# Layer 0 of a two-layer encoder trunk: another order of the inverse's partitions, fewer reads, and roots with reciprocals in PSUM

## The chip, the core and the metric

The kernel runs on one core of a Trainium2 chip. The core has a TensorE (matrix products, written PE; its weight loads are PEld), a VectorE (DVE), a ScalarE (ACT), a GpSimd (POOL) and a SyncE (SP), which here issues nearly all DMAs. Each engine has its own instruction queue and works through it in order; engines wait for each other by semaphores. SBUF is the on-chip memory of 128 partitions, PSUM the accumulator memory that TensorE writes. The metric is the device time of one execution in microseconds (us). Lower is better.

## The reference

The reference is one inference step of a trunk with two layers, for a prompt of 512 tokens and a sample of 32 tokens that carries state. Layer 0 mixes tokens by an RWKV-7 recurrence, layer 1 by differential attention; both also have memory attention and a gate, and one output projection.

What matters for the change is layer 0's recurrence over 24 heads of size 64:

```python
kk = kk / jnp.maximum(jnp.linalg.norm(kk, axis=-1, keepdims=True), 1e-12)
...
sa = jnp.einsum('bhvk,bhk->bhv', S, -kk_t)
S = (S * w_t[:, :, None, :] + sa[..., None] * (kk_t * a_t)[:, :, None, :]
     + v_t[..., None] * k_t[:, :, None, :])
y_t = jnp.einsum('bhvk,bhk->bhv', S, r_t)
...
y = (y - mean) * lax.rsqrt(var + GN_EPS) * ln_w + ln_b
```

The kernel handles it by chunks of 64 tokens. Inside a chunk the `sa` rows depend on each other through a strictly triangular matrix, so the kernel needs the inverse of a unit triangular matrix of 64 by 64 for each chunk and head. It inverts the diagonal blocks of 32 by 32 by elimination and joins two of them by products. It also needs two kinds of inverse square roots: of the norms of `kk`, and of the variances of `y`.

## The kernel before

The 24 heads are worked through as 12 pairs (two heads fill 128 partitions). While the chunk chain of pair `pr` runs, the kernel prepares pairs `pr + 1` to `pr + 3` and finishes pair `pr - 1`. All of it is interleaved by hand with the big matrix products of the input projection, which are done in three passes of float32r (`hh*whi`, `hl*whi`, `hh*wlo`); these fill TensorE wherever the chain leaves room. Each product's result is a half of a block, 128 by 272, accumulated in a PSUM buffer named `ps_g`, from a ring of three buffers (`psg`); ScalarE and VectorE empty it.

The order of layer 0 is written out: `PLAN` has, for each of the 24 steps of a pair's chain, what is done beside it; `Queue` and `tie` chain the instructions of TensorE, VectorE, ScalarE and SyncE in the order in which the program issues them. GpSimd's instructions are not chained in this way; they are placed by the framework's scheduler. In layer 1 the scheduler orders all engines.

The steps that matter here are:

- `rw_prep` makes a pair's triangular blocks `at` and writes the blocks to be inverted to DRAM as `sc1`: 34 blocks of 32 by 32 (32 of the prompt, 2 of the sample).
- "inv" is `rw_invert`: SyncE reads `sc1` into the tile `m3` on 102 partitions, each block three times (three classes, `NCL`), and GpSimd runs the elimination: each block's 32 columns are divided among the three classes (column `n` belongs to class `n mod 3`), and 31 steps of a product into `tm` (L861) and a sum into `u3` (L863) follow. `u3` starts as a copy of `ui`, which holds ones at each class's columns.
- "back" is `rw_back`: SyncE writes `u3` to DRAM (`sc2`), class by class. "at" is `rw_at`: SyncE reads it back into `at`. "mrg" is `rw_merge`: VectorE transposes blocks into `t1b`, TensorE joins two inverted blocks (`ps_w`), ScalarE copies.
- "rsq" computes both kinds of roots in one call: `q20` is a tile of 128 by 26, 16 columns of sums of squares of `kk` from `rw_prep` and 10 columns of variances from `rw_finish`; the result is `r20`. In the profile both have the name `q`, and the temporary tile is `nt`. The call is `self.rsqrt` with eight VectorE instructions, each of which reads what the one ahead of it wrote. It happens 16 times: once for each of the first three pairs in the lead-in, once in step 17 of each of the 12 chains, and once in the tail.
- "fin" is `rw_finish`: after "rsq" comes the multiplication of `yt` by `r20` on VectorE, then TensorE's transposes into `ps_y`, then the gate. Also `rw_prep` reads `r20`: it splits 16 columns into `rr`, which TensorE transposes into `ps_rt`.

Before the change the three classes of the 32 prompt blocks lie on partitions 0 to 31, 32 to 63 and 64 to 95, and those of the two sample blocks on 96 to 101. So `rw_invert` issues six DMAs, two for each class. `consts_rwkv` builds the class of each partition, `cls`, by five comparisons of the partition's number with 32, 64, 96, 98 and 100, and from it `ui`.

`self.rsqrt` begins with an estimate from the exponent bits and has two polynomial steps. Other calls of it (input norms, layer 1) are not touched.

The tail of layer 0 (`TAIL`) is one more "rsq" and the last "fin" steps, in the middle of the last gate's product; directly after it the output projection starts, which opens two `ps_g` buffers at once.

Of the kernel before, what the change touches and what calls it, by code (L numbers as in the profile page):

```python
# [9 lines left out]
F32 = mybir.dt.float32  # L10
F32R = mybir.dt.float32r
BF16 = mybir.dt.bfloat16
I32 = mybir.dt.int32
AF = mybir.ActivationFunctionType
ALU = mybir.AluOpType
AX = mybir.AxisListType

P = 128
# [72 lines left out]
NCL = 3  # L91
NBLK = 34
# [16 lines left out]
class Trunk:  # L109
# [21 lines left out]
    def rsqrt(self, y, x, pool, tag):  # L131
# [10 lines left out]
        self.ve.scalar_tensor_tensor(t[:], t[:], -10.0 / 3.0 * f ** 2, t[:], ALU.add, ALU.mult)  # L142
        self.ve.scalar_tensor_tensor(y, t[:], 5.0 * f ** 4, y, ALU.add, ALU.mult)

    def params(self, p, name, rows, queue=None):

        t = p.tile([P, P], F32, name=name)
        r0 = 0
        for src, n in rows:
            (queue or self.se).dma_start(t[r0 : r0 + n, :], src)  # L150
            r0 += n
        return t, r0
# [34 lines left out]
    def consts_rwkv(self, c):  # L187

        nc, a = self.nc, self.a

        mk = c.tile([P, 2, P], BF16, name="mk")
        self.mk = mk
        nc.gpsimd.memset(mk[:], 1.0)
        for par in range(2):
            for half in range(2):
                strict = (half == 1) if par == 0 else (half == 0)
                for rb in (0, 64):
                    v = mk[rb : rb + 64, par, half * 64 : half * 64 + 64]
                    nc.gpsimd.affine_select(
                        out=v, in_=v, pattern=[[1, 64]], compare_op=ALU.is_gt if strict else ALU.is_ge,  # L200
                        fill=0.0, base=0, channel_multiplier=-1)

        self.hsel = c.tile([P, 34], F32, name="hsel")
        nc.gpsimd.memset(self.hsel[:], 0.0)
        nc.gpsimd.memset(self.hsel[:64, 2:3], 1.0)
        nc.gpsimd.memset(self.hsel[64:, 3:4], 1.0)
        self.hblk = c.tile([P, P], F32, name="hblk")
        nc.gpsimd.memset(self.hblk[:], 0.0)
        nc.gpsimd.memset(self.hblk[:64, :64], 1.0)
        nc.gpsimd.memset(self.hblk[64:, 64:], 1.0)  # L210

        self.hs4 = c.tile([P, 5, P], F32R, name="hs4")
        t4 = self.rp.tile([P, 5, P], F32, tag="rkv", name="t4", bufs=RKV)
        for c0, n, base in ((0, 4, 0), (4, 1, -2)):
            nc.gpsimd.iota(t4[:, c0 : c0 + n], pattern=[[-4, n], [-1, 2], [0, 64]], base=base, channel_multiplier=1,
                           allow_small_or_imprecise_dtypes=True)
        t5 = self.rp.tile([P, 5, P], F32, tag="rkv", name="t5", bufs=RKV)
        self.ve.tensor_scalar(t5[:], t4[:], 0.0, None, ALU.is_equal)
        self.ve.scalar_tensor_tensor(self.hs4[:], t4[:], float(NS), t5[:], ALU.is_equal, ALU.add)

        self.smask = c.tile([P, CW], BF16, name="smask")
        nc.gpsimd.memset(self.smask[:], 1.0)
        nc.gpsimd.memset(self.smask[:].rearrange("p (c w) -> p c w", w=65)[:, :, 0:1], 0.0)

        nr = (32 + NCL - 1) // NCL
        self.nr = nr
        self.ui = c.tile([NCL * NBLK, nr, 32], BF16, name="ui")
        ii = self.rp.tile([NCL * NBLK, nr, 32], F32, tag="rkv", name="ii", bufs=RKV)

        cl = c.tile([NCL * NBLK, 1], F32, name="cl")  # L230
        nc.gpsimd.iota(cl[:], pattern=[[0, 1]], base=0, channel_multiplier=1, allow_small_or_imprecise_dtypes=True)
        cls = c.tile([NCL * NBLK, 1], F32, name="cls")
        self.ve.tensor_scalar(cls[:], cl[:], 32.0, None, ALU.is_ge)
        for at, w in ((64, 1.0), (96, -2.0), (98, 1.0), (100, 1.0)):
            cl2 = c.tile([NCL * NBLK, 1], F32, name=f"cl{at}")
            self.ve.tensor_scalar(cl2[:], cl[:], float(at), None, ALU.is_ge)
            self.ve.scalar_tensor_tensor(cls[:], cl2[:], w, cls[:], ALU.mult, ALU.add)
        nc.gpsimd.iota(ii[:], pattern=[[NCL, nr], [-1, 32]], base=0, channel_multiplier=0,
                       allow_small_or_imprecise_dtypes=True)
        self.ve.tensor_scalar(self.ui[:], ii[:], cls[:, 0:1], 0.0, ALU.add, ALU.is_equal)  # L240
        self.SB = [[c.tile([P, P], F32, name=f"SB{i}{j}") for j in range(2)] for i in range(2)]
        self.SS = [c.tile([P, P], F32, name=f"SS{i}") for i in range(2)]
        for t in self.SB + [self.SS]:
            for u in t:
                nc.gpsimd.memset(u[:], 0.0)
        self.shc = c.tile([P, 2, NPROJ], F32, name="shc")
        self.nlam = self.c.tile([P, 1], F32, name="nlam")

        for t in self.zr[:2] + [self.bk]:
            self.pads(t)  # L250
        nc.gpsimd.memset(self.avz[:], 0.0)
        for t in self.svs:
            nc.gpsimd.memset(t[:], 0.0)
        nc.gpsimd.memset(self.q20[:], 1.0)
        nc.gpsimd.memset(self.uz[:].bitcast(F32), 0.0)
        nc.gpsimd.memset(self.rr[:].bitcast(F32), 0.0)
# [584 lines left out]
    def rw_invert(self, st):  # L841

        nc, p, sc1 = self.nc, self.rb, st["sc1"]
        if st["pr"] == 1:
            m3 = self.sg2[: NCL * NBLK, :1024].rearrange("p (s t) -> p s t", t=32)
            u3 = self.rk0.tile([P, 10, 64], F32, tag="gsq", name="u3r", bufs=1)
            u3 = u3[: NCL * NBLK].rearrange("p a b -> p (a b)")[:, : self.nr * 32].rearrange("p (n t) -> p n t", t=32)
        else:
            m3 = p.tile([NCL * NBLK, 32, 32], F32, tag="m3", name="m3", bufs=1)[:]
            u3 = p.tile([NCL * NBLK, self.nr, 32], F32, tag="u3", name="u3", bufs=1)[:]  # L850
        st["u3"] = u3
        for q in range(NCL):
            self.se.dma_start(m3[q * 32 : q * 32 + 32], sc1[:32])
            self.se.dma_start(m3[96 + 2 * q : 98 + 2 * q], sc1[32:])
        nc.gpsimd.tensor_copy(u3, self.ui[:])
        tm = p.tile([NCL * NBLK, self.nr, 32], F32, tag="tm", name="tm", bufs=1)
        for kx in range(31):
            n = kx // NCL + 1
            wd = 31 - kx
            sh = [NCL * NBLK, n, wd]  # L860
            nc.gpsimd.tensor_tensor(tm[:, :n, :wd], u3[:, :n, kx : kx + 1].to_broadcast(sh),  # L861
                                    m3[:, kx : kx + 1, kx + 1 :].to_broadcast(sh), ALU.mult)
            nc.gpsimd.tensor_tensor(u3[:, :n, kx + 1 :], u3[:, :n, kx + 1 :], tm[:, :n, :wd], ALU.add)  # L863

    def rw_back(self, st):

        u3 = st["u3"]
        st["sc2"] = [self.dp.tile([m, 32, 32], F32, tag=f"sc2{m}", name=f"sc2{m}", bufs=2) for m in (32, 2)]
        for o, t in zip((0, 96), st["sc2"]):
            m = t.shape[0]  # L870
            for q in range(NCL):
                n = len(range(q, 32, NCL))
                self.se.dma_start(t[:, q : 32 : NCL, :], u3[o + q * m : o + q * m + m, :n, :])

    def rw_at(self, st):

# [557 lines left out]
    def layer0(self, mem):  # L1434
        nc, o = self.nc, self.o
        w = self.a["rw_in"][0]
# [4 lines left out]
        with ExitStack() as ctx:  # L1441
# [23 lines left out]
            def go(kind, pr):  # L1465

                if kind == "rsq":
                    self.rsqrt(self.r20[:], self.q20[:], self.rk0, "nt")
                elif 0 <= pr < NPAIR:
                    if kind in ("inv", "back", "at"):  # L1470
                        {"inv": self.rw_invert, "back": self.rw_back, "at": self.rw_at}[kind](sts[pr])
                        return
                    if (kind, pr) not in run:
                        it = run[kind, pr] = self.rw_prep(sts[pr], rkv[pr]) if kind == "prep" else make[kind](sts[pr])
                        next(it)
                    next(run[kind, pr], None)
# [96 lines left out]
            for k, n in enumerate(FILL0):  # L1573
                go("prep", 0)
                if k == 3:
                    go("rsq", 0)
                if k == 26:
                    go("inv", 0)
                fill(n)
# [27 lines left out]
            for pr in range(NPAIR):  # L1607
# [9 lines left out]
                t, left, spent = 0.0, each[pr] - kept, 0.0  # L1617
# [56 lines left out]
        with ExitStack() as ctx:  # L1674
            p = self.pool("wo0", 1, ctx=ctx)
# [66 lines left out]
            for i in range(5):  # L1742
                n = P if i < 4 else TS
                dg = p.tile([P, P], F32, tag="dg", name="dg", bufs=2)
                self.ve.tensor_scalar(dg[:], self.ident[:], rs[:, i : i + 1], None, ALU.mult)
                c = i % 4 * P
# [490 lines left out]
```

## Time and profile before

| | |
|---|---|
| median of 3 runs | 1403.26 us (1402.6 to 1403.94) |
| the profiled execution: its time, its span | 1402.28 us, 1400.5 us |
| TensorE busy | 1361.5 us, 97% of the span |
| VectorE, ScalarE, GpSimd busy | 934.6, 828.6, 371.7 us |
| layer 0, about | 0 to 705 us of the span |
| granted TensorE clock | 0.996 |

How to read it: a row of a timeline has the start in us from the span's start, the duration in us, the engine, the line, the operation, the tiles as out<-in, the shape, and in square brackets the idle time of the engine just before it with what ended it. Nearly all instructions bear the line L106, that of the helper that issues them, so tiles' names tell them apart. A row of waits has the engine and tile that waited, what it waited for, and then us in total, times, and the longest in us. A group's row ends with its count, total busy us and mean ns of one. In a row by tile the three numbers are the shortest, median and longest duration in ns. SPq is SyncE's queue, with the time that it took to issue a DMA. Matmuls overlap, so two rows of PE can cover the same time.

### The profile page before, as it was taken

Reading aid. Unit: us, or ns where it says so; the run is one execution under the profiler, and the core shown is the slowest. Engines: PE = TensorE matmul, PEld = TensorE weight load, DVE = VectorE, ACT = ScalarE, POOL = GpSimd, SP = SyncE. Lnnn points to the kernel's source line nnn. Section 1 sums busy time; section 2 is a strip of 40 time slices with the busy share of each in tenths; the row PEclk is TensorE's granted clock in tenths of the full one; section 3 lists DMA queues with packets and bytes.
Section 4 is the critical chain, followed back from the end, with each engine's and each line's share of the span. In section 5 each row is a group of like instructions: output and inputs, shape, how many; then the busy total and the mean of one; then the engine's idle time right before and its main releaser. Section 6 shows DMA issues by size and latency. Waiting matters only on the chain.

```text
span 1400.5 us, 31939 instructions
## 1 busy us (share of the span) xinstructions
PE 1361.5 (97%) x11893; PEld 1296.7 (93%) x11893; DVE 934.6 (67%) x2345; ACT 828.6 (59%) x2304; POOL 371.7 (27%) x841
## 2 busy tenths in 40 slices
PE   8999999999999999999999999999999999999997
PEld 6988899999998998897899999999999999999997
DVE  5765777787877787676753476676467756767443
ACT  5756677767776777565543366664466546665222
POOL 2136567555865576520000040000000001001000
PEclk9999999999999999999999999999999999999999
DMA  7543222332233222342474473333333322332321
GB/s 224 155 118 80 49 57 76 84 96 62 67 82 99 61 77 73 87 131 64 121 206 118 120 218 108 92 92 93 101 92 94 104 73 84 97 106 84 91 76 72
DMA packets 264036, 139.45 MB, mean 100 GB/s; under 512 B 57721, under 2 KB 252802, under 8 KB 263882
## 3 DMA queue, kind: packets, MB, share of 16 engines
q1 hardware_dynamic: 263818, 137.41, 34.9%
q8 instruction: 94, 1.54, 0.5%
q14 instruction: 60, 0.49, 0.1%
q10 hardware_dynamic: 64, 0.02, 0.0%
HBM read 111.12 MB, written 22.91 MB: 96 GB/s over the span
## 4 chain that ended last, share of the span: by engine, by line
PE 81%; DVE 8%; ACT 3%; issue 2%; POOL 2%; DMA 2%; SPq 1%; DVEq 0%; ACTq 0%; POOLq 0%
PE ps_g L106 57%; PE ps_c L106 4%; PE ps_s L106 2%; PE ps_o L106 2%; PE ps_at L106 2%; DVE wlo L106 1%; PE ps_v L106 1%; SPq L106 1%; PE ps_mm L106 1%; PE ps_mo L106 1%; POOL tm L861 1%; PE ps_aT L106 1%; PE ps_yc L106 1%; POOL u L863 1%; PE ps_kv L106 1%
## 5 line engine op out<-in xcount | busy, mean ns | idle before, releaser
L106 PE MATMUL ps_g<-hh,whi 128*128 128x272 f32 x1808 | 541.0, 300 | 0.4 <-DVE memk L106 0.2
L106 PE MATMUL ps_g<-hh,wlo 128*128 128x272 f32 x1808 | 536.0, 297 | 1.6 <-DVE wlo L106 1.6
L106 PE MATMUL ps_g<-hl,whi 128*128 128x272 f32 x1808 | 532.1, 295 | 0.6 <-DVE hl L106 0.3
L106 PEld LDWEIGHTS ps_g<-hh,wlo 128*128 128x128 f32 x1808 | 341.7, 189 | 6.3 <-DVE wlo L106 2.3
L106 PEld LDWEIGHTS ps_g<-hh,whi 128*128 128x128 f32 x1808 | 341.9, 189 | 5.8 <-DVE og L106 0.6
L106 PEld LDWEIGHTS ps_g<-hl,whi 128*128 128x128 f32 x1808 | 341.8, 189 | 4.6 <-DVE hl L106 1.3
L106 DVE TENSOR_TENSOR wlo<-raw,whi 128x512 fp32r<-128x512 f32 x314 | 220.9, 714 | 123.0 <-ACT whi L106 119.2
L106 ACT CAST whi<-raw 128x512 fp32r<-128x512 f32 x314 | 189.1, 619 | 109.5 <-PE ps_g L106 61.4
L861 POOL TENSOR_TENSOR tm<-u,m 102x84 f32<-102x84 f32 (+23 forms) x341 | 143.7, 421 | 165.5 <-DMA m<-sc 139.7
L863 POOL TENSOR_TENSOR u<-u,tm 102x84 f32<-102x84 f32 (+23 forms) x341 | 148.3, 435 | 26.6
L106 PE MATMUL ps_g<-hi,whi 128*128 128x272 f32 x512 | 148.9, 291 | 0.0
L106 PE MATMUL ps_g<-hi,wlo 128*128 128x272 f32 x512 | 147.5, 288 | 0.5 <-DVE wlo L106 0.5
L106 PE MATMUL ps_g<-lo,whi 128*128 128x272 f32 x512 | 147.4, 288 | 0.0
L1333 POOL TENSOR_TENSOR lo<-og,hi 128x544 fp32r<-128x544 f32 x8 | 13.2, 1652 | 359.7 <-ACT hi L106 359.2
L106 PEld LDWEIGHTS ps_g<-hi,wlo 128*128 128x128 f32 x512 | 96.4, 188 | 0.8 <-DVE wlo L106 0.7
L106 PEld LDWEIGHTS ps_g<-hi,whi 128*128 128x128 f32 x512 | 96.4, 188 | 0.0
L106 PEld LDWEIGHTS ps_g<-lo,whi 128*128 128x128 f32 x512 | 96.4, 188 | 0.0
L106 ACT ACTIVATE pt<-ps_s,snm 128x128 f32<-128x128 f32 (+3 forms) x96 | 51.0, 532 | 41.7 <-DVE snm L106 41.6
L106 DVE SCALAR_TENSOR_TENSOR SB<-ps_c,dl,sd 64x64 f32<-64x64 f32 x168 | 47.4, 282 | 40.9 <-PE ps_c L106 37.7
L1754 POOL TENSOR_TENSOR hl<-hn,hh 128x544 fp32r<-128x544 f32 x8 | 12.5, 1567 | 211.3 <-ACT hh L106 211.2
L106 ACT ACTIVATE sg<-ps_g 128x272 f32<-128x272 f32 x64 | 25.3, 396 | 57.6 <-PE ps_g L106 53.0
L106 ACT COPY sv<-ps_c 64x64 f32<-64x64 f32 x192 | 39.5, 206 | 33.3 <-PE ps_c L106 31.2
(402 smaller groups left out, 2578.3 us busy)
## 6 DMA issues: line engine op xcount, KB each, us to landing
raw<-in_rw_in_dram SPq DMA_DIRECT2D x114, 256.0 KB
raw<-in_df_in_dram SPq DMA_DIRECT2D x112, 256.0 KB
raw<-in_w_out_dram SPq DMA_DIRECT2D x64, 256.0 KB
oscr<-sg SPq DMA_DIRECT2D x16, 272.0 KB
lo<-oscr SPq DMA_DIRECT2D x16, 272.0 KB
m<-sc SPq DMA_DIRECT2D x33, 128.0 KB
raw<-in_w_mem_v_dram SPq DMA_DIRECT2D x16, 256.0 KB
kh<-kh SPq DMA_DIRECT2D x24, 136.0 KB
```

Of the source, the lines that this page charges most:

```text
L106: return lambda *a, **k: self.trunk.tie(self, issue(*a, **k))
L861: nc.gpsimd.tensor_tensor(tm[:, :n, :wd], u3[:, :n, kx : kx + 1].to_broadcast(sh), m3[:, kx : kx + 1, kx + 1 :].to_broadcast(sh), ALU.mult)
L863: nc.gpsimd.tensor_tensor(u3[:, :n, kx + 1 :], u3[:, :n, kx + 1 :], tm[:, :n, :wd], ALU.add)
L1333: (self.nc.gpsimd if g % 2 and self.o1 else self.ve).tensor_tensor(lo[:], t, hi[:].bitcast(F32), ALU.subtract)
L1754: nc.gpsimd.tensor_tensor(self.hl[:, k, :], h[:], self.hh[:, k, :].bitcast(F32), ALU.subtract)
```

## The change

Three parts.

1. A block's three classes move to neighbouring partitions: partition `3 b + q` has class `q` of block `b`. `m3` is then read by two DMAs (prompt blocks and sample blocks), whose source repeats each block three times by a step of nothing. `rw_back` still issues six DMAs; each takes every third partition.
2. `consts_rwkv` gets `cls` in another way: two iotas on GpSimd write, for each partition, its distances from the starts of the blocks 1 to 33 into the tile `ii`; VectorE compares them with 0, sums them over the row, and so has the block's number; a third instruction gets the class. After that `ii` is written again, as before, for `ui`.
3. "rsq" calls the new `roots`. With x the input, u an estimate of the square root of x from its exponent bits, s = u + x/u (twice a Heron step), the result is about 1/s + s/(4 x), with a small factor on each part. The instructions are eight, on VectorE alone: the seed; `z` = 1/x; `w` = 1/u; `d` = `w` x; `u` = `d` + `u`; `w` = 1/`u`; `u` = 0.25 (1 - m) `u` `z`; out = (1 + m) `w` + `u`. `z`, `w` and `d` lie in PSUM, in a buffer of the ring `psg` in which the matrix products accumulate.

```diff
+    def roots(self):
+
+        x, out = self.q20[:], self.r20[:]
+        n = x.shape[1]
+        u = self.rk0.tile([P, n], F32, tag="nt", name="nt")[:]
+        ps = self.psg.tile([P, 512], F32, tag="g", name="ps_nt")
+        z, w, d = (ps[:, i * n : i * n + n] for i in range(3))
+        m = 3.0e-4
+        self.ve.tensor_scalar(u.bitcast(I32), x.bitcast(I32), 0.5, float(0x1FBB4F2E), ALU.mult, ALU.add)
+        self.ve.reciprocal(z, x)
+        self.ve.reciprocal(w, u)
+        self.ve.tensor_tensor(d, w, x, ALU.mult)
+        self.ve.tensor_tensor(u, d, u, ALU.add)
+        self.ve.reciprocal(w, u)
+        self.ve.scalar_tensor_tensor(u, u, 0.25 * (1.0 - m), z, ALU.mult, ALU.mult)
+        self.ve.scalar_tensor_tensor(out, w, 1.0 + m, u, ALU.mult, ALU.add)
...
         cls = c.tile([NCL * NBLK, 1], F32, name="cls")
-        self.ve.tensor_scalar(cls[:], cl[:], 32.0, None, ALU.is_ge)
-        for at, w in ((64, 1.0), (96, -2.0), (98, 1.0), (100, 1.0)):
-            cl2 = c.tile([NCL * NBLK, 1], F32, name=f"cl{at}")
-            self.ve.tensor_scalar(cl2[:], cl[:], float(at), None, ALU.is_ge)
-            self.ve.scalar_tensor_tensor(cls[:], cl2[:], w, cls[:], ALU.mult, ALU.add)
+        nc.gpsimd.iota(ii[:, 0, :], pattern=[[-NCL, 32]], base=-NCL, channel_multiplier=1, allow_small_or_imprecise_dtypes=True)
+        nc.gpsimd.iota(ii[:, 1, 0:2], pattern=[[-NCL, 2]], base=-33 * NCL, channel_multiplier=1,
+                       allow_small_or_imprecise_dtypes=True)
+        jj = ii[:].rearrange("p n t -> p (n t)")[:, : NBLK - 1]
+        self.ve.tensor_scalar(jj, jj, 0.0, None, ALU.is_ge)
+        self.ve.tensor_reduce(cls[:], jj, AX.X, ALU.add)
+        self.ve.scalar_tensor_tensor(cls[:], cls[:], -float(NCL), cl[:], ALU.mult, ALU.add)
         nc.gpsimd.iota(ii[:], pattern=[[NCL, nr], [-1, 32]], base=0, channel_multiplier=0,
                        allow_small_or_imprecise_dtypes=True)
         self.ve.tensor_scalar(self.ui[:], ii[:], cls[:, 0:1], 0.0, ALU.add, ALU.is_equal)
...
-        for q in range(NCL):
-            self.se.dma_start(m3[q * 32 : q * 32 + 32], sc1[:32])
-            self.se.dma_start(m3[96 + 2 * q : 98 + 2 * q], sc1[32:])
+        for b in (slice(0, 32), slice(32, NBLK)):
+            self.se.dma_start(m3[b.start * NCL : b.stop * NCL],
+                              sc1[b].unsqueeze(1).to_broadcast([b.stop - b.start, NCL, 32, 32]))
...
-                self.se.dma_start(t[:, q : 32 : NCL, :], u3[o + q * m : o + q * m + m, :n, :])
+                self.se.dma_start(t[:, q : 32 : NCL, :], u3[o + q : o + NCL * m : NCL, :n, :])
...
                 if kind == "rsq":
-                    self.rsqrt(self.r20[:], self.q20[:], self.rk0, "nt")
+                    self.roots()
```

## The prediction

> **What bounds the kernel now.** I read the page's busy line first, then the waits of TensorE, then the timeline around the longest class of them.
>
> ```profile
> span 1400.5 us, 31939 instructions
> ```
>
> ```profile
> PE 1361.5 (97%) x11893; PEld 1296.7 (93%) x11893; DVE 934.6 (67%) x2345; ACT 828.6 (59%) x2304; POOL 371.7 (27%) x841
> ```
>
> TensorE is the bound: it is busy for 1361.5 of 1400.5 us. None of the edits touches a matmul, so all they can win or lose lies in the other 39 us, where TensorE stood still. The view of waits says who held it:
>
> ```profile
> PE ps_y L106 <- DVE yt L106: 5.0, 10, 0.9
> PE ps_rt L106 <- DVE rr L106: 2.8, 1, 2.8
> PE ps_w L106 <- DVE t1b L106: 2.5, 5, 1.1
> ```
>
> All three stand behind something that the change touches. `ps_y` holds the transposes of a finished pair's outputs; they need `yt`, which VectorE multiplies by the roots `r20`, straight after the step "rsq". `ps_w` begins the merge of two inverted blocks, which waits for the inverse to come back from DRAM. VectorE's timeline in pair 1 and the TensorE row that waits for it:
>
> ```profile
> 208.14 0.17 DVE L106 TENSOR_SCALAR q<-gs 128x10 f32<-128x10 f32 x1
> 208.25 0.69 DVE L106 TENSOR_TENSOR wlo<-raw,whi 128x512 fp32r<-128x512 f32 x1
> ...
> 214.40 0.17 DVE L106 TENSOR_SCALAR q<-q 128x26 int32<-128x26 int32 x1
> ...
> 215.96 0.19 DVE L106 SCALAR_TENSOR_TENSOR q<-nt,q 128x26 f32<-128x26 f32 x1
> 216.06 0.73 DVE L106 TENSOR_TENSOR wlo<-raw,whi 128x512 fp32r<-128x512 f32 x1
> 216.72 0.85 DVE L106 TENSOR_TENSOR yt<-yt,q 128x640 f32<-128x640 f32 x1
> ```
>
> ```profile
> 217.72 0.74 PE L106 MATMUL ps_y<-ident,yt 128*128 128x128 f32 x5 [0.35 <-DVE yt L106]
> ```
>
> VectorE has no gap from 214.40 to the end of `yt` at 217.57, and TensorE resumes 0.15 us later after 0.35 us of waiting. So here the length of the roots sets when TensorE goes on, one to one. It is worse where GpSimd's elimination runs beside them (stretches of pair 1 and of a later pair, from the first to the last instruction of the roots; the columns are us, then PE, PEld, DVE, ACT and POOL busy):
>
> ```profile
> 214.40:216.15 1.75, 1.75 (x17) 1.75 (x16) 1.51 (x10) 1.68 (x6) 0.96 (x4) 1.00 0.20 55
> 443.37:445.41 2.04, 2.04 (x20) 2.04 (x18) 1.80 (x10) 1.97 (x7) 1.65 (x6) 1.00 0.14 40
> ```
>
> ```profile
> 447.14 0.63 PE L106 MATMUL ps_y<-ident,yt 128*128 128x128 f32 x4 [0.88 <-DVE yt L106]
> ```
>
> The same eight instructions take 1.75 us with 0.96 us of GpSimd beside them and 2.04 with 1.65, and TensorE's wait is 0.35 in the one and 0.88 in the other.
>
> **The change part by part.**
>
> **1. The roots.** Eight instructions before, eight after. Before, each waits for the one in front: 214.40 to 215.96 is seven steps of 0.22 us, the last ends 0.19 later, 1.75 in all. An instruction that waits for nothing starts after 0.11 (208.14 to 208.25). After: seed, `z`=1/x, `w`=1/u, `d`, `u`, `w`=1/u, `u`·`z`, out. `z` doesn't need the seed, and `u`·`z` doesn't need the second `w`. With old lengths that is five dependent steps (seed to `w`, `w` to `d`, `d` to `u`, `u` to `w`, `u`·`z` to out) of 0.22, one free step of 0.11 and an end of 0.19: 5 x 0.22 + 0.11 + 0.19 = 1.40; `z` lies inside the seed's step. Two prices are not in the trace at this size: a reciprocal of 26 columns, and a VectorE write to PSUM.
>
> ```profile
> L106 DVE RECIPROCAL mrs<-mrs 128x2 f32<-128x2 f32 x16 | 2.6, 165 | 6.9 <-ACT mp L106 6.8
> ...
> L106 DVE RECIPROCAL mrs<-mrs 128x1 f32<-128x1 f32 x8 | 1.3, 162 | 3.1 <-ACT mp L106 3.0
> ```
>
> ```profile
> L106 DVE RECIPROCAL mrs<-mrs x24: 152/166/168, 599.1 to 1154.2; 128x2 f32<-128x2 f32 x16, 128x1 f32<-128x1 f32 x8
> ```
>
> ```profile
> L106 DVE TENSOR_TENSOR tm_t<-tm_t,ps_n x4: 156/157/158, 1387.7 to 1393.2; 128x2 f32<-128x2 f32 x2, 128x3 f32<-128x3 f32 x2
> ...
> L106 DVE TENSOR_TENSOR tm_t<-fr x2: 160/161/162, 1388.1 to 1393.0; 128x2 f32<-128x2 f32 x1, 128x3 f32<-128x3 f32 x1
> ```
>
> ```profile
> L106 DVE MEMSET ps_s<- x96: 112/112/112, 844.0 to 1263.5; 64x64 f32 x96
> ```
>
> Mean to mean, a second column costs a reciprocal 3 ns: 165 + 24 x 3 = 237 ns for 26, against 190 for the step's old instruction. At the other end, from the shortest of the group to its longest, it is 16 ns a column: 168 + 24 x 16 = 552 ns. I take the means' side, where the two visible ones add 0.1 at most, and leave the step as it is. An input from PSUM made a multiplication 4 ns shorter (157 against 161), so PSUM reads are taken as equal. A write to PSUM lies between the memset's 112 ns and the old 190; I take the old. If the four writes (`z` is hidden) cost like the memset, three visible ones save 3 x 0.08 and the roots take 1.16. If instructions that touch the same PSUM bank also run one behind the other, `w` waits for `z` (0.11 more) and `u`·`z` for `w` (0.11 more): 1.62.
>
> [...]
>
> The roots stand in front of `yt` twelve times. Between the two stretches above the saving is 1.75 - 1.40 = 0.35 to 2.04 - 1.40 = 0.64, and the wait that it can remove is 0.35 to 0.88: they grow together. The ten waits hold 5.0 us, and I take four fifths of it, 4.0. (None of the new instructions takes two inputs from SBUF; whether that frees them of GpSimd no row shows, and if not, 0.2 of each long wait stays.) What is late next is the chain's own products `ps_c`, whose VectorE work moves forward with `yt`.
>
> **2. The matrices' reads.** SyncE issues six DMAs per pair before, two after, with the same bytes.
>
> ```profile
> 210.47 2.04 SPq L106 DMA_DIRECT2D m<-sc  x6
> ```
>
> ```profile
> 214.95 0.24 POOL L861 TENSOR_TENSOR tm<-u,m 102x31 f32<-102x31 f32 x1 [9.43 <-DMA m<-sc]
> ```
>
> At 2.04 / 6 = 0.34 each, SyncE is free 1.36 us sooner, and GpSimd's elimination, which starts 4.48 us after the first issue, starts up to 1.36 us sooner (nothing sooner if the bytes, not the issues, set it). In steady pairs no TensorE wait hangs on that. It also has a cost: in pair 1 and its like the elimination would then cover all of the roots and `yt`, as it does at 443. I charge 0.1 for three such pairs, 0.3. At the start SyncE is on the path:
>
> ```profile
> 125.58 2.61 SPq L106 DMA_DIRECT2D sg<-sc  x6
> 128.29 2.34 SPq L106 DMA_DIRECT2D sc<-u  x6
> ```
>
> ```profile
> 133.50 0.43 DVE L106 STREAM_TRANSPOSE t1b<-at 32x256 f32<-32x256 f32 x1 [0.53 <-DMA at<-sc]
> ```
>
> ```profile
> 133.98 0.60 PE L106 MATMUL ps_w<-t1b,at 32*32 32x32 f32 x26 [0.47 <-DVE t1b L106]
> ```
>
> Six reads (2.61) stand in front of pair 0's way back; two save 1.74, more than the 0.47 that TensorE waited: 0.5 gained. The longest single wait is also behind SyncE:
>
> ```profile
> 90.60 2.55 SPq L106 DMA_DIRECT2D up<-in_rw_a_up_dram  x2
> 93.20 1.14 SPq L106 DMA_DIRECT2D raw<-in_rw_in_dram  x2
> ```
>
> ```profile
> 96.58 0.62 ACT L106 CAST whi<-raw 128x512 fp32r<-128x512 f32 x1 [1.17 <-DMA raw<-in_rw_in_dram]
> ```
>
> ```profile
> 100.61 0.33 PE L106 MATMUL ps_rt<-ident,rr 128*128 128x128 f32 x1 [2.75 <-DVE rr L106]
> ```
>
> Two small issues took 2.55 us there against 0.68 for two of 0.34; what held them no row of these tells, and with four fewer instructions in front it may fall elsewhere. Between nothing and 1.87 us I take 0.6.
>
> **3. The way back** has the same six DMAs (2.34 us) with the same sizes and another partition step. I cost it at nothing; it stands behind GpSimd's elimination in every pair.
>
> **4. The constants.** Nine small VectorE instructions become three, and GpSimd's iota of `ii` now waits for VectorE, with `ui` behind it.
>
> ```profile
> L106 DVE SCALAR_TENSOR_TENSOR cls<-cl,cls x4: 152/160/160, 43.1 to 43.9; 102x1 f32<-102x1 f32 x4
> ```
>
> ```profile
> L238 POOL IOTA ii<- x1: 468/468/468, 37.2 to 37.2; 102x352 f32 x1
> ```
>
> Six instructions less save 0.7 to 0.9 us; the iota and the way there and back add 0.5 to 0.8. Behind `ui` on VectorE stands the first shifted column. I take nothing, bounds 0.3 either way.
>
> **5. The bank.** The roots take a buffer of the ring of three in which the matmul blocks accumulate. In the pairs a block's half lasts long enough for the roots to be done before the next needs it. At the end of layer 0 it doesn't:
>
> ```profile
> 696.72 0.17 DVE L106 TENSOR_SCALAR q<-q 128x26 int32<-128x26 int32 x1
> ```
>
> ```profile
> 697.40 0.29 PE L106 MATMUL ps_g<-hi,whi 128*128 128x272 f32 x1
> ```
>
> ```profile
> 699.22 0.43 DVE L106 SCALAR_TENSOR_TENSOR sg<-sg,ps_g 128x272 f32<-128x272 f32 x1
> ```
>
> The output projection opens two accumulators there, the second at 697.40, with one buffer free; of the other two, one is the roots' until 696.72 + 1.40 = 698.12, one holds the last gate until 699.65. Cost 0.7, bounds 0 and 2.2 (if it gets the gate's).
>
> **Sum:** 4.0 - 0.3 + 0.5 + 0.6 - 0.7 = 4.1 us less. The profiled execution took 1402.28 us, 1.8 us around its span, and lies 0.98 under the median of the runs. So 1398.2 for such an execution and 1403.26 - 4.1 = **1399.2** for the median.
>
> **The rivals.**
>
> *The bank in a row.* Roots of 1.62: each of ten waits shrinks by 0.13 to 0.42, about 2.3 in all instead of 4.0, and the tail loses 0.2 more: 1401.1. For it: six of the eight instructions touch one tile. Against it: no such pair stands in this trace.
>
> *Slow reciprocals, the slower side.* Three visible reciprocals replace cheap instructions. At 16 ns a column they cost 552 - 190 = 0.36 us each, roots of 1.40 + 3 x 0.36 = 2.48, 0.44 over the worst call of today and 0.73 over the best; ten waits grow by about 0.6 each, two hidden ones appear, and the tail loses 1.1: 1403.26 + 6.6 + 1.8 - 0.8 = 1410.9. It decides from roots of about 1.9 (365 ns a reciprocal, 8 ns a column), where only the start's gain is left and the tail eats it: 1403; slower by over 0.2% from 2.1. For it: the largest reciprocal in the trace has two columns. Against it: the 3 ns between the means. [...]
>
> *Another wait takes its place.* TensorE no longer waits for `yt` but for the next product of the chain, or for weights. Then half of the 4.0 goes: 1401.2, or 1403 if the order of layer 1 comes out worse. For it: `ps_c` has small waits in other places; against it: VectorE runs without a gap through that stretch, so all behind `yt` comes sooner.
>
> **How the numbers follow.** My forecast has 0.54, the bank in a row 0.18, slow reciprocals 0.14, another wait 0.14. About 0.2%, 2.8 us, is what a measurement of this kernel can tell from no change. The forecast is faster but for 0.05; the bank 0.04 faster and 0.14 same; slow reciprocals 0.07 same and 0.07 slower; another wait 0.10 same and 0.04 slower: faster 0.53, same 0.36, slower 0.11. The low end has PSUM writes at the memset's price (all 5.0 of the waits gone) and the 1.87 whole: 5.0 + 0.5 + 1.9 + 0.3 = 7.7, 1395.6. The high end takes in the bank and part of the slow side: 1404.8.
>
> **What would show it.** Right: `ps_y` waits under 1.5 us in total, roots of 1.35 to 1.5 from seed to out wherever GpSimd is, `m<-sc` in some 0.7 us, no wait at the first `ps_w`. Wrong: reciprocals over 300 ns, `ps_y` waits at 5 or more, a new `ps_g` wait at each half behind the roots, or the 2.75 us at `ps_rt` unchanged (then 0.6 less).

## The result: slower, with the profile after

The changed kernel takes 1411.67 us (median of 11 runs) against 1403.2 for the kernel before (11 runs of the same kind): a ratio of 1.0057, 95% interval 1.0045 to 1.0070, some 8 us slower. Forecast was 1399.2, faster, in a range of 1395.6 to 1404.8. The slower rival of the prediction gave 1410.9, which is near, but the experiments below show that most of the loss doesn't come by its way. The granted TensorE clock of the profiled execution is 0.995, against 0.996 before, so the clock isn't the cause.

The head of the page of the kernel after, and its waits of TensorE (us in all, times, longest):

```profile
span 1409.9 us, 31859 instructions
...
PE 1363.6 (97%) x11893; PEld 1297.5 (92%) x11893; DVE 937.1 (66%) x2339; ACT 827.2 (59%) x2304; POOL 369.3 (26%) x843
```

```profile
PE ps_y L106 <- DVE yt L106: 5.2, 10, 0.7
PE ps_q L106 <- POOL rkk L800: 4.3, 8, 0.9
...
PE ps_w L106 <- DVE t1b L106: 3.6, 6, 1.1
...
PE ps_rt L106 <- DVE rr L106: 1.7, 1, 1.7
...
PE ps_g L106 <- DVE q L106: 1.2, 1, 1.2
```

The ten `ps_y` waits that were to go are still there (5.0 before). The row of `ps_q`, which waits for GpSimd's product `rkk`, was one wait of 0.3 us before and is now 4.3. The single `ps_g` at the end of layer 0 is new. `rkk` stands on GpSimd right behind a pair's elimination, so a late `rkk` is a late elimination. The chain that ended last says the same; before (first fence) and after (second), its shares by engine:

```profile
PE 81%; DVE 8%; ACT 3%; issue 2%; POOL 2%; DMA 2%; SPq 1%; DVEq 0%; ACTq 0%; POOLq 0%
```

```profile
PE 65%; POOL 17%; DVE 5%; issue 4%; DMA 3%; ACT 3%; SPq 2%; DVEq 0%; POOLq 0%; ACTq 0%
```

GpSimd, 2% of the chain before, now holds 17% of it. What has become longer there is seen in SyncE's timeline behind one elimination (it ends at 246.95 before and at 246.86 after), and in the start of the next elimination on GpSimd. Before:

```profile
246.98 2.36 SPq L106 DMA_DIRECT2D sc<-u  x6
249.43 0.94 SPq L106 DMA_DIRECT2D raw<-in_rw_in_dram  x2
250.47 1.94 SPq L106 DMA_DIRECT2D sc<-at  x4
...
253.00 1.85 SPq L106 DMA_DIRECT2D at<-sc  x4
...
255.44 2.58 SPq L106 DMA_DIRECT2D m<-sc  x6
```

```profile
260.45 0.24 POOL L861 TENSOR_TENSOR tm<-u,m 102x31 f32<-102x31 f32 x1 [9.45 <-DMA m<-sc]
...
577.12 0.24 POOL L861 TENSOR_TENSOR tm<-u,m 102x31 f32<-102x31 f32 x1 [8.28 <-DMA m<-sc]
```

After:

```profile
246.88 3.89 SPq L106 DMA_DIRECT2D sc<-u  x6
250.88 0.93 SPq L106 DMA_DIRECT2D raw<-in_rw_in_dram  x2
251.90 1.93 SPq L106 DMA_DIRECT2D sc<-at  x4
...
254.42 2.63 SPq L106 DMA_DIRECT2D at<-sc  x4
...
257.63 1.29 SPq L106 DMA_DIRECT2D m<-sc  x2
```

```profile
214.92 0.24 POOL L880 TENSOR_TENSOR tm<-u,m 102x31 f32<-102x31 f32 x1 [8.86 <-DMA m<-sc]
...
261.62 0.24 POOL L880 TENSOR_TENSOR tm<-u,m 102x31 f32<-102x31 f32 x1 [8.97 <-DMA m<-sc]
...
586.57 0.41 POOL L880 TENSOR_TENSOR tm<-u,m 102x31 f32<-102x31 f32 x1 [7.63 <-DMA m<-sc]
```

Read these as a circle: elimination (32 us), way back `sc<-u`, two loads of weights, the next pair's matrices out (`sc<-at`), the inverses in (`at<-sc`), the next matrices in (`m<-sc`), and the next elimination. In the rounds shown SyncE issues this with gaps of only 0.1 us, before as after. So the circle has a length of its own, and the way back lies on it: its six DMAs went from 2.36 to 3.89 us of SyncE, now that they read every third partition. (The longer `at<-sc` after, 2.63, is not the change's: most rounds have 1.85 there, and both kernels have single ones of 2.6 to 3.1.) The reads, two instead of six, went from 2.58 (2.04 in most pairs) to 1.29, but land later behind the last issue: GpSimd starts 2.70 us after it instead of 2.43, and 2.7 to 3.7 instead of 2.1 to 2.5 over these nine pairs. From the elimination that starts at 215 us to the last, eight rounds took 577.12 - 214.95 = 362.2 us before and 586.57 - 214.92 = 371.7 after: 9.5 us, the whole of the loss and a little more. On the mean of the eight, the elimination went from 31.9 to 31.6 us, the way from its end to the first read from 8.8 to 10.5, and the way from there to the next elimination from 4.6 to 4.4: only SyncE's part grew.

The longer time is that of issuing. What waits for the blocks' landing on GpSimd, the copy of `ui` into `u3`, starts 1.2 us after the last issue before and 1.3 after (first row before, second after):

```profile
250.53 0.48 POOL L855 CAST u<-ui 102x352 f32<-102x352 bf16 x1 [2.27 <-DMA sc<-u]
```

```profile
252.06 0.58 POOL L874 CAST u<-ui 102x352 f32<-102x352 bf16 x1 [3.91 <-DMA sc<-u]
```

The roots, from VectorE's timeline after at the place where the prediction showed them before:

```profile
213.25 0.17 DVE L106 TENSOR_SCALAR nt<-q 128x26 int32<-128x26 int32 x1
213.33 0.32 DVE L106 RECIPROCAL ps_nt<-q 128x26 f32<-128x26 f32 x1
213.68 0.32 DVE L106 RECIPROCAL ps_nt<-nt 128x26 f32<-128x26 f32 x1
214.04 0.19 DVE L106 TENSOR_TENSOR ps_nt<-ps_nt,q 128x26 f32<-128x26 f32 x1
214.26 0.19 DVE L106 TENSOR_TENSOR nt<-ps_nt,nt 128x26 f32<-128x26 f32 x1
214.49 0.32 DVE L106 RECIPROCAL ps_nt<-nt 128x26 f32<-128x26 f32 x1
214.84 0.18 DVE L106 SCALAR_TENSOR_TENSOR nt<-nt,ps_nt 128x26 f32<-128x26 f32 x1
215.06 0.18 DVE L106 SCALAR_TENSOR_TENSOR q<-ps_nt,nt 128x26 f32<-128x26 f32 x1
```

They take 2.00 us (213.25 to 215.25), not 1.40, against 1.73 to 2.04 before.

### The profile page after: what moved, and what is told of

Same layout as the page of the kernel before. It is cut to its first block, busy times and chain, and to the rows that moved or that the text cites. A ratio compares the mean times of both kernels' runs of the same rounds, so it can differ in the third digit from the quotient of the medians.

```text
span 1409.9 us, 31859 instructions
## 1 busy us (share of the span) xinstructions
PE 1363.6 (97%) x11893; PEld 1297.5 (92%) x11893; DVE 937.1 (66%) x2339; ACT 827.2 (59%) x2304; POOL 369.3 (26%) x843
## 4 chain that ended last, share of the span: by engine, by line
PE 65%; POOL 17%; DVE 5%; issue 4%; DMA 3%; ACT 3%; SPq 2%; DVEq 0%; POOLq 0%; ACTq 0%
PE ps_g L106 49%; POOL tm L880 8%; POOL u L882 8%; DMA m<-sc 2%; PE ps_s L106 2%; SPq L106 2%; PE ps_o L106 2%; PE ps_c L106 2%; PE ps_mo L106 1%; PE ps_mm L106 1%; DVE wlo L106 1%; PE ps_aT L106 1%; PE ps_q L106 1%; PE ps_kv L106 1%; POOL rkk L800 1%
## 5 line engine op out<-in xcount | busy, mean ns | idle before, releaser
L882 POOL TENSOR_TENSOR u<-u,tm 102x84 f32<-102x84 f32 (+23 forms) x341 | 144.5, 424 | 26.6
```

## The experiments

Each is compared with the kernel before, run on the same chip among the same rounds (its median was 1402.2 to 1402.9 us there); a ratio stands with its 95% interval, and is not exactly that of the two medians. Two theories were on the table: the **circle** (way back in SyncE's queue, above), and the **roots** (three reciprocals of 0.32 us, the prediction's slower rival).

### The roots alone

The kernel before with `roots()` in place of `rsqrt`:

```
-                    self.rsqrt(self.r20[:], self.q20[:], self.rk0, "nt")
+                    self.roots()
```

> The kernel before with the new roots alone; constants, reads and way back as before. The loop theory (a pair of layer 0 is set by GpSimd's elimination and the queue of SyncE behind it, and the stepped way back made that loop longer): the roots are about 2.0 us instead of 1.72 to 2.04, the output projection waits 1.2 us for its second accumulator at the end of layer 0, and `ps_y` waits stay near 5 to 6 us: 1404.5, between 1403.5 and 1406. The roots theory (three reciprocals of 0.32 us are the loss): nearly all of the loss is here, 1409 to 1412.

Measured: 1404.76 us, ratio 1.0018 (1.0009 to 1.0027). The `ps_y` waits rise to 6.8 us and the output projection waits 1.2. So the roots lose 1 to 4 us of the 8; the roots theory, which had 1409 to 1412 here, falls.

### The layout alone

The changed kernel with the old roots, the line above the other way round.

> The changed kernel with the old roots: classes on neighbouring partitions, two reads, stepped way back, new constants. Loop theory: the way back takes 3.9 us of SyncE instead of 2.36, the period from one elimination to the next is 46.2 to 47.4 us instead of 44.7 to 46.4, `ps_q` waits for GpSimd's `rkk` for about 4 us in all: 1410, between 1408 and 1411.5. Roots theory: 1401 to 1403.5.

Measured: 1409.11 us, ratio 1.0048 (1.0033 to 1.0063). The circle's part is the larger one; with the 2.5 us of the roots alone the two parts make 9.2 (0.18 and 0.48% of 1402.4 are 2.5 and 6.7), the measured whole of 8 within their intervals. Its waits of TensorE:

```profile
PE ps_w L106 <- DVE t1b L106: 4.9, 5, 2.0
PE ps_q L106 <- POOL rkk L800: 4.8, 6, 1.3
...
PE ps_y L106 <- DVE yt L106: 2.9, 10, 0.4
```

`ps_y` waits are shorter than before (2.9 against 5.0) though nothing was done for them: the elimination starts later in the round, after the roots, which so take 1.71 to 1.81 us.

### The way back without its step

The changed kernel, with the way back reading runs of neighbouring partitions:

```
-                self.se.dma_start(t[:, q : 32 : NCL, :], u3[o + q : o + NCL * m : NCL, :n, :])
+                self.se.dma_start(t[:, q : 32 : NCL, :], u3[o + q * m : o + q * m + m, :n, :])
```

> The changed kernel with the way back reading runs of neighbouring partitions (so that blocks and classes are mixed up: the inverses that come back are not those of their blocks; sizes and number of DMAs are the same). Loop theory: the way back takes 2.4 us of SyncE again, the periods are those of before, `ps_q` waits for `rkk` go: 1404.5, between 1402.5 and 1406, as the roots alone. If the step isn't what costs (the reads' broadcast or the roots are): 1410 to 1412.

Measured: 1403.79 us, ratio 1.0010 (1.0001 to 1.0018). The row of the way back is the old one:

```profile
245.66 2.34 SPq L106 DMA_DIRECT2D sc<-u  x6
```

Each against its own runs of the kernel before, the loss falls from 0.57% to 0.10%: one step in one access pattern is some 6.6 us of the 8. Two reads instead of six, the broadcast and the new constants, which this kernel still has, show no loss or gain beside the roots alone (1.0010 and 1.0018).

### Two reads in the old order of partitions

The kernel before with the reads alone changed, so that the way back keeps its runs:

```
-        for q in range(NCL):
-            self.se.dma_start(m3[q * 32 : q * 32 + 32], sc1[:32])
-            self.se.dma_start(m3[96 + 2 * q : 98 + 2 * q], sc1[32:])
+        for b in (slice(0, 32), slice(32, NBLK)):
+            self.se.dma_start(m3[b.start * NCL : b.stop * NCL],
+                              sc1[b].unsqueeze(0).to_broadcast([NCL, b.stop - b.start, 32, 32]))
```

> The kernel before with two reads per pair instead of six, each class still a run of 32 (or 2) partitions and the way back as before. If the bytes set when the elimination starts: SyncE is done some 0.75 us sooner, GpSimd starts 3.9 to 4.6 us after the first issue as now, 1402 to 1404. If the issues set it: each pair's loop is up to 0.75 us shorter, until TensorE's own work is the bound, 1398 to 1401.

Measured: 1444.92 us, ratio 1.0301 (1.0282 to 1.0321). Neither expectation holds, and the run doesn't answer the question it was made for. SyncE's row of the reads and the next elimination on GpSimd:

```profile
268.66 1.55 SPq L106 DMA_DIRECT2D m<-sc  x2
```

```profile
279.25 0.24 POOL L861 TENSOR_TENSOR tm<-u,m 102x31 f32<-102x31 f32 x1 [15.04 <-DMA m<-sc]
```

GpSimd starts 9.04 us after the last issue (279.25 - 270.21) instead of 2.43. With the three copies outermost, the trace has 2.7 of the 4 KB packets in flight at a time on the mean, over 7.6 us; in the changed kernel, where 32 blocks are outermost, 10.5 over 1.8 us. For the circle theory it is a test with a larger dose: the way from one elimination's end to the next start is 19.1 us here (279.25 - 260.19) instead of 13.5, the circle 49.9 us instead of 45.5, `ps_q` waits 23.6 us in all, and the kernel is 42 us longer. TensorE's granted clock also falls where it waits so much (0.97 between 200 and 300 us, 1.00 before), but the parts of this round on GpSimd and SyncE follow each other with gaps of only 0.1 us up to the last read's issue, so the longer round is the reads' landing.

### A class's 34 blocks as one run

The kernel before with three reads and three writes back of 34 rows (and the constants for this order):

```
+            self.se.dma_start(m3[q * NBLK : q * NBLK + NBLK], sc1[:])
...
+            self.se.dma_start(sc2[:, q : 32 : NCL, :], u3[q * NBLK : q * NBLK + NBLK, :n, :])
```

> The kernel before with a class's 34 blocks on neighbouring partitions: three reads of 34 rows and three writes back of 34 rows, none stepped or repeated, instead of six and six; old roots. If issues set the loop of GpSimd and SyncE: it is 2 us shorter per pair, and what TensorE has to do sets the pair: 1398 to 1402. The other outcome, from the run with two reads (reads over three copies landed 8.3 to 9.3 us after the last issue, as if three of the DMA engines carried 32 packets of 159 ns each): if 34 rows go over 2 engines, 51 packets of 159 ns are 8.1 us on each, periods of about 50 us and 1435 to 1455. [...]

Measured: 1474.12 us, ratio 1.0501 (1.0488 to 1.0515): the second outcome in kind, but 19 us over its range.

```profile
268.39 3.77 SPq L106 DMA_DIRECT2D sc<-u  x3
...
279.74 0.88 SPq L106 DMA_DIRECT2D m<-sc  x3
```

```profile
290.68 0.33 POOL L859 TENSOR_TENSOR tm<-u,m 102x31 f32<-102x31 f32 x1 [13.94 <-DMA raw<-in_rw_in_dram]
```

The three issues of the reads are cheap, but GpSimd starts 10.1 us after them (290.68 - 280.62); 2.0 of the packets are in flight at a time, over 9.2 us. No run shows that 34 rows go over 2 engines, as the expectation had it; shown are the mean numbers of packets in flight, 2.0 here against 2.7 and 10.5 above, and packets over 9.2 us where my estimate had 8.1. The way back has grown here too, to 3.77 us of SyncE for three DMAs of neighbouring rows, so a step over partitions is not the only thing that makes an issue long, and this run doesn't price the reads alone. The split of 34 into 32 and 2 in the reads and writes is worth more here than the issues it costs: without it the median was 1474.12 us against 1402.85.

### What the roots are made of

First the temporaries in SBUF instead of PSUM, in the tiles of the result and of the argument (in part, and against the roots alone, as the next edit is):

```
-        self.ve.reciprocal(z, x)
-        self.ve.reciprocal(w, u)
-        self.ve.tensor_tensor(d, w, x, ALU.mult)
...
+        self.ve.reciprocal(out, u)
+        self.ve.tensor_tensor(out, out, x, ALU.mult)
...
+        self.ve.reciprocal(out, x)
+        self.ve.reciprocal(x, u)
```

> The kernel before with the new roots, their reciprocals and their product in SBUF (in the tiles of the roots and of their argument) instead of a buffer of PSUM. If the reciprocal itself costs 6 ns a column: it takes 310 to 330 ns here too, the roots take 2.0 us alone and up to 2.4 beside GpSimd, `ps_y` waits grow from 6.8 to about 8 us in all, and the 1.2 us of the output projection go: 1404.5, between 1403 and 1406.5. If it is the write to PSUM that makes it long: 190 to 240 ns, roots of 1.6 to 1.8 us, 1400 to 1402.5.

Measured: 1405.15 us, ratio 1.0015 (1.0006 to 1.0023); `ps_y` waits 8.7 us in all, and the output projection's wait is gone, since no buffer of PSUM is taken. Then the eight instructions with no reciprocal among them:

```
-        self.ve.reciprocal(z, x)
-        self.ve.reciprocal(w, u)
+        self.ve.tensor_scalar(z, x, 0.0, 0.05, ALU.mult, ALU.add)
+        self.ve.tensor_scalar(w, u, 0.0, 0.05, ALU.mult, ALU.add)
...
```

> The roots alone, each of the three reciprocals replaced by a multiplication and addition with constants in the same places (so that all roots are one constant: left out is the computation of the roots, not its eight instructions). If the prediction's step 1 was wrong in the reciprocal's length alone: roots of 1.45 to 1.6 us, `ps_y` waits of 1 to 2 us in all instead of 6.8, the output projection waits 0.6 to 0.8 us instead of 1.2: 1399.5, between 1398 and 1401.5. If another wait takes its place (the chain's products, GpSimd and SyncE's queue): `ps_y` waits fall all the same and the time stays at 1402 to 1404.

Measured: 1400.27 us, ratio 0.9981 (0.9972 to 0.9990). VectorE's groups of the changed kernel, of the SBUF form and of the form without reciprocals (count, then busy us and mean ns of one):

```profile
L106 DVE RECIPROCAL ps_nt<-nt 128x26 f32<-128x26 f32 x32 | 10.4, 324 | 1.1
```

```profile
L106 DVE RECIPROCAL q<-nt 128x26 f32<-128x26 f32 x32 | 10.1, 317 | 1.1
```

```profile
L106 DVE TENSOR_SCALAR ps_nt<-nt 128x26 f32<-128x26 f32 x32 | 6.0, 189 | 1.1
```

A reciprocal of 26 columns is 317 ns in SBUF and 324 into PSUM, so the length is the operation's: against the 165 ns of two columns it is (317 - 165) / 24 = 6.3 ns a column. Without the three the roots take 1.59 to 1.65 us in the pairs' chains, `ps_y` waits fall from 6.8 to 2.1 us, and the kernel is 1.4 to 3.9 us faster than before. So the saving the prediction wanted was to be had from shorter roots; these were not shorter.

Beside GpSimd's elimination only the first instruction of the roots, the one with both ends in SBUF, becomes longer (up to 283 ns instead of 173 in the run with the roots alone), and they take 2.0 to 2.1 us whether GpSimd runs or not; the SBUF form takes 2.1 to 2.3, and the old roots 1.73 to 2.04. That PSUM is what spares the other seven isn't shown: the reciprocals with both ends in SBUF keep their length too (316 to 318 ns), and of the SBUF form's other instructions only some become longer, and in some pairs (0.25 and 0.28 us beside 0.19 for two others, in the pair at 260.5 us).

### TensorE's order and the circle, each alone and both

What bounds a pair if not one thing? In the kernel before, the multiplication of `yt` was put straight behind the roots, ahead of a low half of weights that had stood between them:

```
-    [[("prep", 3, 0.11, 0.17), ("mrg", 1, 0.9, 0)], [("rsq", 0, 0, 1.5)]],
-    [[("prep", 3, 0.33, 0)], [("fin", -1, 0, 0.88)]],
+    [[("prep", 3, 0.11, 0.17), ("mrg", 1, 0.9, 0)], [("rsq", 0, 0, 1.5), ("fin", -1, 0, 0.88)]],
+    [[("prep", 3, 0.33, 0)], []],
```

> The kernel before, old roots, with the multiplication of `yt` ordered straight behind the roots, ahead of the low half of the weights that stood between them in each pair. If VectorE's order is what TensorE waits for: `yt` is 0.7 us sooner, the `ps_y` waits (5.0 us) go, 1399, between 1397 and 1401. If the low halves of the weights are then late (`ps_g` waits for `wlo` at each pair) or GpSimd's loop with SyncE is what sets a pair: 1402 to 1406.

Measured: 1404.37 us, ratio 1.0008 (0.9998 to 1.0017). All `ps_y` waits are gone, and nothing is won. The view of the tile `ps_q` lists what TensorE's matmuls and weight loads waited for before it (us, times); its row for `rkk` in the kernel before, in this one, and in the changed kernel:

```profile
  POOL rkk L781: 0.9, 2
```

```profile
  POOL rkk L781: 6.1, 11
```

```profile
  POOL rkk L800: 10.2, 16
```

With `ps_y` gone, TensorE waits for `rkk` instead: the circle lay close behind TensorE's own order all the time. But not all of the 5 us is seen there again. The rows above count weight loads too; of the matmuls alone, `ps_q` waits for `rkk` rise from 0.3 to 2.4 us. The circle also grew in this run, from 45.3 to 45.6 us a round, with eliminations of 32.4 us instead of 31.9 on the mean; why these are longer no run shows. Late weights are not it: the `ps_g` waits for `wlo` are 2.5 us, against 2.4 before. Next, the circle shortened: the four writes of the next pair's matrices, in the round above ready two microseconds before the elimination ends, go ahead of the way back, into time in which SyncE waits for GpSimd.

```
+        sc1 = self.dp.tile([NBLK, 32, 32], F32, tag="sc1", name="sc1", bufs=2)
+        for e in range(2):
+            for b in range(2):
...
+                self.se.dma_start(sc1[n : n + 8].rearrange("b s t -> s b t"), ...)
         yield
         st["ats"] = ats = self.rb.tile([P, 2, 2, 64], F32, tag="ats", name="ats", bufs=2)
...
```

> The kernel before with the four writes of the next pair's matrices (`sc<-at`, 2.0 us of SyncE) issued ahead of the way back, so that they go out while SyncE waits for GpSimd. The theory of two bounds (the loop of GpSimd and SyncE and TensorE's own order are within half a microsecond of each other per pair): the loop is 2 us shorter, `ps_y` still waits 5 us, so little is won: 1402, between 1400 and 1403.5. If the loop alone sets a pair: 1390 to 1397.

Measured: 1402.14 us, ratio 1.0009 (1.0000 to 1.0017): nothing won here either, as `ps_y` still waits 5.7 us. In five of eight rounds the matrices are not ready so early, and the way back then starts 0.9 to 2.7 us after the elimination's end, where it started at once before; so the circle doesn't win all of the 2 us. Both edits together, in the kernel before:

> The kernel before with both: `sc<-at` ahead of the way back, and `yt` straight behind the roots. Two bounds: `yt` first alone won nothing since `ps_q` then waited for GpSimd's `rkk`; with the loop 2 us shorter it keeps its 5 us: 1397.5, between 1395.5 and 1400. If something else holds TensorE (the weights' low half, the chain's products): 1401 to 1404.

Measured: 1399.83 us, ratio 0.9986 (0.9973 to 0.9998). Neither edit wins alone; together they win a little, some 2 us and less than the 5 expected. SyncE's timeline in this kernel:

```profile
241.72 1.82 SPq L106 DMA_DIRECT2D sc<-at  x4
244.73 2.32 SPq L106 DMA_DIRECT2D sc<-u  x6
...
248.68 1.85 SPq L106 DMA_DIRECT2D at<-sc  x4
...
251.07 2.10 SPq L106 DMA_DIRECT2D m<-sc  x6
```

`m<-sc` is issued 6.3 us after the way back (251.07 - 244.73) instead of 8.5 (255.44 - 246.98), and TensorE no longer waits at `ps_y`, nor at `ps_q` for `rkk`. Last, the same two in the changed kernel:

> The changed kernel with `sc<-at` ahead of the way back. Two bounds: the 2.0 us taken from the loop cover the 1.5 that the stepped way back adds; the `rkk` waits go and the loss of the new roots is left: 1404, between 1402.5 and 1406. If the stepped way back costs by anything else than its place in the queue of SyncE ahead of the next reads: 1408 to 1412.

> The changed kernel with `sc<-at` ahead of the way back and `yt` straight behind the roots. Two bounds: all that is left of the change's loss is the output projection's wait of 1.2 us at the end of layer 0 and the 0.2 us of the roots in the first pairs: 1399, between 1397 and 1401.5. If the long roots cost by more than the wait for `yt`: 1402 to 1406.

Measured: 1403.16 us, ratio 1.0009 (1.0000 to 1.0018), with the writes ahead; 1401.22 us, ratio 0.9990 (0.9981 to 0.9998), with both. With the writes ahead alone, the way back is as long as in the changed kernel, and the `rkk` waits are down to 0.3 us:

```profile
245.45 3.87 SPq L106 DMA_DIRECT2D sc<-u  x6
```

```profile
PE ps_y L106 <- DVE yt L106: 6.4, 10, 0.7
...
PE ps_q L106 <- POOL rkk L800: 0.3, 1, 0.3
```

With the circle relieved the stepped way back, still there, costs nothing that can be told; with `yt` first the long roots cost nothing that can be told either, but for the 1.2 us at the output projection. Both losses are so tied to their places.

## Why the prediction was wrong

Two terms failed, and each makes about half of the 12 us between forecast and result. The way back, put at nothing, cost some 6.6 us; the roots, forecast to win 4.0 and to pay 0.7 at their bank, lost 2.5. Each alone makes the kernel slower, as the layout alone and the roots alone show.

**The step that failed first: "I cost it at nothing; it stands behind GpSimd's elimination in every pair."** Two errors are in it. The first is the price: same number, same sizes, another partition step, and 3.89 us instead of 2.36, 0.26 more for each DMA on the mean. With the step taken out, the loss fell from 0.57% to 0.10%. The row before showed only unstepped ones, and I took the step as free without a bound, while I gave bounds to the reads. The second is the place. Behind the elimination is not off the path: the trace of the kernel before already showed that SyncE goes from the way back to the next reads without a gap, and that the next elimination waits for these. The same error stands in step 2, "In steady pairs no TensorE wait hangs on that". No wait of TensorE hung on it because the circle (45.3 us a round) was a hair shorter than TensorE's pair (45.9, from the `ps_y` at 217.72 to that at 447.14, five pairs on); a wait that isn't there says nothing about how much room there is. The room had to be worked out: the sum of a round on GpSimd and SyncE against the pair on TensorE.

**1. The roots**, the second term that failed. 1.40 forecast, 2.00 measured. The reciprocal is 324 ns, not 190: three times 0.13 is 0.40. It was mis-sized by choosing the step between two means (3 ns a column) over the other end (16); 6.3 is between them. The other 0.2 is from the two instructions that I had as free. `u`·`z` writes `u` over what the second `w` reads, so it has to wait for it (it starts at 214.84, the second `w` ends at 214.81): an oversight in reading the code. (In the SBUF form, which uses no PSUM, the second and third reciprocals also overwrite what the one ahead reads, and each starts 0.03 us after that one's end.) And `w` waits for `z`, though it needs only the seed (`z` ends at 213.65, `w` starts at 213.68): in the trace's records the seed gives no signal of its own, and that of `z`, which comes after it, stands for both. Without reciprocals the eight take 1.59, close to the 1.62 of the rival "the bank in a row"; the two waits named here account for it with no bank, though no run has the bank apart. That the ten waits shrink with the roots, one to one, held: `ps_y` went 6.8 to 2.1 us as the roots went from 2.0 to 1.6, and the ratio from 1.0018 to 0.9981.

**2. The reads.** Two issues cost 1.29 us, not 0.68, since each takes 0.65. That the start of the elimination gains "nothing sooner if the bytes, not the issues, set it" was a bound, and it is what happened. The 0.3 charged for more overlap with the roots has the wrong sign: the elimination came later, not sooner, and in the layout alone the roots were freed of it. Nor did the start gain: the way back of pair 0 is 3.92 us there instead of 2.34, and the first `ps_w` waits 0.66 us instead of 0.47. The 2.75 us at `ps_rt` are 1.67 now, but 1.8 to 2.8 in the runs above with six reads too, so this is not the change's.

**4. The constants** cost nothing, as taken. **5. The bank:** the place and the mechanism were right, the size follows the roots. The second accumulator waits until the last root instruction is done:

```profile
706.50 0.18 DVE L106 SCALAR_TENSOR_TENSOR q<-ps_nt,nt 128x26 f32<-128x26 f32 x1
```

```profile
706.74 0.39 PE L106 MATMUL ps_g<-hi,whi 128*128 128x272 f32 x1 [1.21 <-DVE q L106]
```

1.21 us instead of 0.7, as the roots are 0.6 longer.

**The rivals and signs.** Two of the signs named for being wrong came: reciprocals of 317 to 324 ns, and `ps_y` waits of 5.2 us. "Slow reciprocals" had the right direction, roots of 2.48 where 2.00 were measured, and 1410.9: a time that agrees with the measured one by chance. By its own point ("it decides from roots of about 1.9") roots of 2.00 would have been slightly slower than before, and the roots alone were that, 1404.8. "Another wait takes its place" named the chain's products; the wait that does so is `ps_q`, on GpSimd and SyncE. None of the rivals had the way back.

Still open is why SyncE needs 0.26 us more to issue a DMA whose SBUF side steps over partitions, and about as much for the reads that repeat a block; it wasn't tried with other steps. Nor is it known why three writes of 34 neighbouring rows took 3.77 us.

## What to carry to other kernels

When two engines take turns, add up the round (work, issues, landings) and set it beside the bound engine's own time per stage before calling anything on it free: with half a microsecond of room a round, an edit on one side shows only until the other side binds. Here two edits that won nothing each won some 2 us together, while shorter roots alone could win 1.4 to 3.9. Read what a DMA costs its queue by its pattern, not by its bytes: a step over partitions in SBUF or a repeated source in DRAM was some 0.3 us an issue here, and with 3 and 34 rows outermost in reads of the same 408 KB the elimination started 9.0 and 10.1 us after their last issue, against 2.7 with 32. Cost an instruction at its real number of columns, and look which operand of a "free" one overwrites what its neighbour still reads.

## What the runs showed of the hardware that was not expected

- A DMA of 32, or of 2, partitions that steps by three partitions took SyncE 0.57 to 0.64 us to issue, against 0.27 to 0.46 in a run of partitions (medians); the surcharge is 0.30 to 0.31 us for 2 partitions and 0.15 to 0.29 for 32 (six of them 3.89 against 2.36 us).
- The mean number of packets in flight was 10.5 with 32 rows outermost in the read, 2.7 with 3 and 2.0 with 34, and the elimination that waits for these reads, of the same 408 KB, started 2.7, 9.0 and 10.1 us after their last issue.
- A reciprocal on VectorE cost 6.3 ns a column between two columns and 26 (165 and 317 ns), where a multiplication of 26 columns is 189 in all.
- In the new roots, VectorE's instructions with one side in PSUM kept their length beside GpSimd's elimination (181 to 325 ns, each to within 10), while the first, with both sides in SBUF, grew from 173 to as much as 283 ns. A reciprocal with both sides in SBUF kept its length as well.
